# Neighbourhood attention: key windows of 23, 31, 31 and 24 columns, and the upper left tiles' keys in two blocks of partitions

## The chip, the cores and the metric

The kernel runs on one core of a Trainium2 chip. The core has five engines that run side by side, each with its own queue of instructions: TensorE (PE: matrix products and transposes into PSUM), VectorE (DVE), ScalarE (ACT), GpSimd (POOL) and SyncE (SP, which here only issues transfers). The metric is the time of one execution on the device in microseconds, lower is better; from several runs the median is taken.

## The reference

One layer of an encoder on 1024 tokens, a grid of 16 rows and 64 columns, in float32. The input is normalised and projected; half of the projected columns feed a gated convolution over positions, the other half a two-dimensional neighbourhood attention with 8 heads of 64. Both results are projected together and added to the input, and a gated feed-forward part follows. What matters here is the attention:

```python
def row_block(r):
    row_start = jnp.clip(r - kh // 2, 0, rows - kh)              # kh = 8 rows
    q_r = lax.dynamic_index_in_dim(qg, r, axis=1, keepdims=False)
    k_rows = lax.dynamic_slice_in_dim(kg, row_start, kh, axis=1)
    v_rows = lax.dynamic_slice_in_dim(vg, row_start, kh, axis=1)
    k_win = k_rows[:, :, col_idx]      # 16 columns from clip(col - 8, 0, 48)
    v_win = v_rows[:, :, col_idx]
    s = jnp.einsum("bqhd,brqchd->bhqrc", q_r, k_win) * scale
    s = s + bias                       # a learned bias for each offset
    p = jax.nn.softmax(s, axis=(-2, -1))
    return jnp.einsum("bhqrc,brqchd->bqhd", p, v_win)
```

A query in row r and column c attends to 8 rows by 16 columns, 128 keys; near the edges the window is pushed inside the grid.

## The kernel before

The layer runs in stages on one core: the input projections (keys, gate and convolution input, queries, values), the attention, the output projection, the feed-forward part's first two products and its last one. The convolution's taps run on VectorE, ScalarE and GpSimd beside TensorE's projections. The order of all instructions is the order in which the program writes them (a manual schedule); each engine takes its own in that order and waits where data or a buffer isn't there yet.

The attention takes the queries in eight tiles of 8 rows by 16 columns, 128 queries each: `rh` is the upper (0) or lower (1) half, `cb` the column block from 0 to 3. A tile's keys are a rectangle that holds the windows of all its queries: 12 rows (`AR`) from row `4 * rh` on, and the columns of `WIN[cb]`, a first column and a count. Keys outside a query's own window get a bias of -1e30 and so a weight of zero. The tiles go in the order (0,0), (1,0), (0,3), (1,3), (0,1), (1,1), (0,2), (1,2); with four pairs of heads each they make 32 units, `i` from 0 to 31. Units 0 to 3 are the upper left tile (0,0), 4 to 7 the lower left, 8 to 15 the tiles of column block 3, and 16 to 31 the wide ones of blocks 1 and 2. A unit's steps:

- `score_mm` (L646): the product of queries and keys for each of two heads, one PSUM bank each of 288 or 384 columns. In the trace that is 4 instructions, as a float32 product is two.
- `score_exp`: for each head VectorE adds the bias table and finds the maximum (L659), ScalarE takes the exponential with its sum (L661).
- `score_norm`: VectorE inverts the sums (L666), GpSimd multiplies (L668).
- `flip` (L677): TensorE transposes the weights, so that keys lie on partitions. With 288 keys that is three blocks of 96 for each head, with 384 three of 128, so 6 transposes. They go to a PSUM buffer of which there is one (`cv`).
- `flip_out` (L682): the second head's block is copied to SBUF by ScalarE, the first's by VectorE.
- `weigh` (L693): three products with the values for each head, which add up in PSUM; 12 instructions.

The loop works in a skewed order. Its step `i` issues the score of unit `i`, the normalisation of unit `i - 1`, the flip of `i - 2` and the weighing of `i - 3`. Beside these, odd steps below 19 hold four transposes of the convolution's result (L793) with its statistics (L802) and a copy (L806); steps 18 to 22 an inverse root on VectorE (L816 and on); steps 23 to 30 the scaling of the convolution's result (`conv_scale`, L824); steps 17 to 32 splits of output weights into two parts (L114, L118) and steps 15, 25 and 30 an accumulating load by GpSimd (L148). Units 0 and 1 have their scores earlier, ahead of the last two value projections (L122 to L124, `z`).

The values go to a DRAM buffer `vd` as they come, two grid rows a step (L434, issued by ScalarE). `load_vw` (L631, on SP) brings them back as one tile for each group of four rows: the rectangle's keys on partitions, 96 or 128 of them. Upper tiles use groups 0 to 2, lower ones 1 to 3. Two groups share one of 22 SBUF buffers of 4 KB a partition (`G`), which nearly everything else in the attention uses as well; a buffer that is given back goes to the next that asks.

The bias tables are built in DRAM much earlier. `t1` has one for each of three kinds of column block (left, inner, right), `tf` one for each kind and half; `fill1` and `fill2` fill them with -1e30, `run` writes the biases in runs of 16, `rows_of` copies 8 rows for a row of queries. `table` (L619, on SP) loads one for a tile.

Of the kernel before, what the change touches and what calls it, by code (L numbers as in the profile page):

```python
# [6 lines left out]
F32 = mybir.dt.float32  # L7
# [6 lines left out]
P = 128  # L14
# [4 lines left out]
NH = 8  # L19
HD = 64  # L20
# [3 lines left out]
EPS = 1e-6  # L24
NEG = -1e30
GW = 64
AR = 12
SIDE = ((16, 17, 18, 19, 20, 21, 22),) * 2 + ((16, 17, 18, 19, 20, 21, 22, 23, 24),) + (tuple(range(16, 28)),)
WIN = ((0, 24, 8), (8, 32, 0), (24, 32, 0), (40, 24, 0))


def layout(v):
# [42 lines left out]
def build(ctx, tc, a):  # L75
    nc = tc.nc
    pe, act, dve, pool = nc.tensor, nc.scalar, nc.vector, nc.gpsimd
# [3 lines left out]
    dr = ctx.enter_context(tc.tile_pool(name="dr", bufs=1, space=bass.MemoryType.DRAM))  # L81
# [4 lines left out]
    def G(name, dt=F32):  # L86
        return T("G", [P, 1024], 22, name, dt)
# [16 lines left out]
    def mm(name):  # L104
        return ps.tile([P, 512], F32, tag="mm", bufs=4, name=name)
# [142 lines left out]
    for kp in range(4):  # L248
        load_xt(0, kp, FIRST)
        if kp < 3:  # L250
# [15 lines left out]
                       base=0, channel_multiplier=1)  # L266
    qgs = T("qgs", [P, 1], 1, "qgs")
    dve.tensor_scalar(qgs, qg, HD ** -0.5, None, op0=OP.mult)
    t1 = [dr.tile([NH, 16, 15, ncol], F32, name=f"t1{ty}") for ty, ncol in enumerate((24, 32, 24))]
    tf = {(rh, ty): dr.tile([8, 16, NH, AR * t1[ty].shape[-1]], F32, name=f"tf{rh}{ty}")  # L270
          for rh in range(2) for ty in range(3)}

    def rstd_of(ss, scale, name):
# [222 lines left out]
    def bias_tables():  # L496
        neg = G("neg")
        pool.memset(neg, NEG)

        def fill1(ty):  # L500
            n = 15 * t1[ty].shape[-1]
            nc.sync.dma_start(t1[ty].rearrange("h j u b -> (h j) (u b)"), neg[:, :n])

        def fill2(rh, ty):
            n = 3 * AR * t1[ty].shape[-1] if ty != 1 else 2 * AR * 32
            for o in range(0, NH * AR * t1[ty].shape[-1], n):
                w = min(n, NH * AR * t1[ty].shape[-1] - o)
# [100 lines left out]


    def table(rh, ty):  # L610
        n = AR * t1[ty].shape[-1]
        src = tf[rh, ty].rearrange("i j h c -> (i j) (h c)")
        if rh == 0 and ty == 0:
            parts = [(G(f"tab{k}")[:, :n * min(3, NH - 3 * k)], 3 * k) for k in range(3)]
        else:
            parts = [(H(f"tab{rh}{ty}")[:, :NH * n], 0)]
        heads = []
        for w, h0 in parts:
            nc.sync.dma_start(w, src[:, h0 * n:h0 * n + w.shape[-1]])  # L619
            heads += [w[:, o:o + n] for o in range(0, w.shape[-1], n)]  # L620
        return heads
# [2 lines left out]
    vwt, vw = {}, {}  # L624

    def load_vw(cb, g):
        c0, ncol, _ = WIN[cb]
        if g % 2 == 0:
            vwt[cb, g // 2] = G(f"vw{cb}{g}").rearrange("p (g d) -> p g d", d=512)
        vw[cb, g] = vwt[cb, g // 2][:4 * ncol, g % 2, :]  # L630
        nc.sync.dma_start(vw[cb, g], vd.rearrange("(r c) d -> r c d", c=GW)[g * 4:g * 4 + 4, c0:c0 + ncol, :])  # L631


    k4 = kT.rearrange("p c (r w) -> p c r w", w=GW)
    order = [(rh, cb) for cb in (0, 3, 1, 2) for rh in range(2)]
# [2 lines left out]
    def score_mm(i):  # L638
        s_, hp = divmod(i, 4)
        rh, cb = order[s_]  # L640
        t = rh * 4 + cb
        c0, ncol, _ = WIN[cb]
        out = []
        for hh in range(2):
            s = mm(f"s{i}{hh}")[:, :AR * ncol]
            pe.matmul(s, qT[hh * HD:(hh + 1) * HD, hp, t * P:(t + 1) * P],  # L646
                      k4[hh * HD:(hh + 1) * HD, hp, rh * 4:rh * 4 + AR, c0:c0 + ncol], start=True, stop=True)
            out.append(s)
        return out

    def score_exp(i, ss):
        s_, hp = divmod(i, 4)
        rh, cb = order[s_]
        n = AR * WIN[cb][1]
        e = es[i] = G(f"e{i}").rearrange("p (h n) -> p h n", h=2)[:, :, :n]
        rs = SM(f"rs{i}", 2)
        for hh in range(2):
            mx = SM(f"mx{i}{hh}", 1)
            dve.tensor_tensor_reduce(out=e[:, hh], in0=ss[hh], in1=tab[rh, cb][2 * hp + hh], scale=-1.0,  # L659
                                     scalar=3.0e38, op0=OP.add, op1=OP.min, accum_out=mx)  # L660
            act.activation(e[:, hh], e[:, hh], AF.Exp, bias=mx, scale=-1.0, accum_out=rs[:, hh:hh + 1])  # L661
        sums[i] = rs
# [6 lines left out]

    def flip(i):  # L670
        s_, hp = divmod(i, 4)
        m = 4 * WIN[order[s_][1]][1]
        pp[i] = cv(f"p{i}")
        for hh in range(2):
            pt = pp[i][:, hh * 512:hh * 512 + 384]
            for g in range(3):
                pe.transpose(pt[:m, g * P:(g + 1) * P], es[i][:, hh, g * m:(g + 1) * m], ident)  # L677
        pTs[i] = G(f"pT{i}").rearrange("p (n h q) -> p n h q", h=2, q=P)[:m, :3]

    def flip_out(i, hh):  # L680
        m = pTs[i].shape[0]
        (dve.tensor_copy, act.copy)[hh](pTs[i][:, :, hh], pp[i][:m, hh * 512:hh * 512 + 384].rearrange(  # L682
            "p (n q) -> p n q", q=P))

    def weigh(i):
        s_, hp = divmod(i, 4)
        rh, cb = order[s_]
        if hp == 0:
            os_[s_] = tp(f"o{s_}").rearrange("p (c q) -> p c q", c=4)
        for g in range(3):  # L690
            for hh in range(2):
                c = (2 * hp + hh) * HD
                pe.matmul(os_[s_][hh * HD:(hh + 1) * HD, hp], vw[cb, rh + g][:, c:c + HD], pTs[i][:, g, hh],  # L693
                          start=g == 0, stop=g == 2)

    rowf, diff, a11 = [], [], {}

# [55 lines left out]
    load_window(3)  # L753
    tab[1, 3] = table(1, 2)

# [645 lines left out]
```

## Time and profile before

| | |
|---|---|
| median of 3 runs | 1049.9 us (1049.48 to 1050.58) |
| the profiled execution | 1050.14 us |
| its span, first to last instruction | 1048.4 us |
| TensorE busy | 1028.2 us, 98% |
| VectorE, ScalarE, GpSimd busy | 722.9, 465.3, 452.6 us |
| clock granted to TensorE | 0.999 of full |
| scores L646, flips L677, weighings L693 on TensorE | 26.73, 28.54, 28.04 us busy |

The span is what the trace covers; the execution's own time is 1.7 us longer. Times in the trace count from the span's start. The units' scores begin between 227 and 315 us, and the last weighing begins at 325. "Busy" of a group is the time in which at least one of its instructions runs: TensorE's overlap, so that the mean length of one is more than its share. "Idle before" is the time in which the engine stood still just ahead of an instruction, with what released it.

### The profile page before, as it was taken

To read this page: it belongs to the slowest core of one execution; us is meant where nothing else is said; L and a number is where in the kernel's file an instruction comes from. 1 tells how busy PE (TensorE), PEld (TensorE's weight loads), DVE (VectorE), ACT (ScalarE), POOL (GpSimd) and SP (SyncE) were. 2 spreads that over 40 slices of the span, in tenths; PEclk is the share of its full clock that TensorE was granted. 3 is DMA by queue.
4 is the path that set the end of the run, shared out by engine and by line. 5 is a ranking of instruction groups with operands and counts; after the bars stand their busy time and mean duration, and the time that the engine had idled before them with its cause. 6 is when DMAs were issued, how large, how long until landed. Compare 5 with 4: busy or idle time off the path is not lost.

```text
span 1048.4 us, 13903 instructions
## 1 busy us (share of the span) xinstructions
PE 1028.2 (98%) x4972; PEld 833.8 (80%) x4972; DVE 722.9 (69%) x1097; ACT 465.3 (44%) x915; POOL 452.6 (43%) x342
## 2 busy tenths in 40 slices
PE   7999999999999999999999999999999999999997
PEld 5888888776657888778888888888888888888885
DVE  6768998976896575876564655646556567768883
ACT  6466346636776676532232232232322443443441
POOL 0226578833575863655545454455454100002310
PEclk9999999999999999999999999999999999999999
DMA  9496771285536754465232132232232597633641
GB/s 334 178 271 220 225 238 61 77 244 168 148 109 163 159 182 141 109 167 174 104 131 101 71 131 101 89 132 93 99 111 81 207 326 256 205 101 125 215 133 40
DMA packets 74678, 162.93 MB, mean 155 GB/s; under 512 B 13489, under 2 KB 22193, under 8 KB 73905
## 3 DMA queue, kind: packets, MB, share of 16 engines
q1 hardware_dynamic: 67776, 144.14, 40.7%
q0 software_dynamic: 4864, 10.49, 5.9%
q10 hardware_dynamic: 1968, 7.42, 2.0%
q8 instruction: 39, 0.64, 0.2%
q14 instruction: 31, 0.25, 0.1%
HBM read 122.86 MB, written 53.15 MB: 168 GB/s over the span
## 4 chain that ended last, share of the span: by engine, by line
PE 88%; DVE 4%; POOL 2%; DMA 2%; ACT 2%; issue 2%; SPq 0%; POOLq 0%; ACTq 0%; DVEq 0%
PE B L122 5%; PE B L123 5%; PE B L124 5%; PE D L123 4%; PE D L124 4%; PE D L122 4%; PE A L122 3%; PE A L123 3%; PE A L124 3%; PE z L123 3%; PE z L122 3%; PE z L124 3%; PE gl L124 3%; PE gl L123 3%; PE gl L122 3%; PE n L122 3%
## 5 line engine op out<-in xcount | busy, mean ns | idle before, releaser
L347 DVE SCALAR_TENSOR_TENSOR cv<-u,par,cv 128x1009 f32<-128x1009 f32 (+14 forms) x85 | 108.5, 1276 | 2.0
L373 POOL TENSOR_TENSOR pa<-pa,pr 128x1022 f32<-128x1022 f32 (+10 forms) x31 | 75.2, 2426 | 33.7 <-ACT pr L372 32.2
L1356 POOL TENSOR_TENSOR ou<-ou,resm 128x512 f32<-128x512 f32 x8 | 12.5, 1571 | 142.5 <-DMA resm<-xd 142.5
L114 ACT CAST op<-sr 128x512 fp32r<-128x512 f32 x77 | 47.7, 619 | 52.7 <-PE B2d L124 21.3
L118 DVE TENSOR_TENSOR op<-sr,op 128x512 fp32r<-128x512 f32 x77 | 58.2, 756 | 16.4 <-ACT op L114 16.4
L1193 DVE TENSOR_TENSOR g<-B,g 128x512 f32<-128x512 f32 x22 | 15.2, 690 | 71.3 <-PE B L124 68.2
L1202 ACT ACTIVATE D<-D 128x512 f32<-128x512 f32 x22 | 12.8, 582 | 112.5 <-DVE D L1201 112.5
L1185 DVE TENSOR_TENSOR u<-B,g 128x512 f32<-128x512 f32 x22 | 15.2, 691 | 61.0 <-PE B L124 61.0
L668 POOL TENSOR_SCALAR e<-e,rs 128x288 f32<-128x288 f32 (+1 forms) x64 | 35.0, 568 | 45.6 <-DVE rs L666 41.0
L114 ACT CAST op<-wd 128x512 fp32r<-128x512 f32 x66 | 40.9, 620 | 30.4 <-DVE wd L1280 17.4
L118 DVE TENSOR_TENSOR op<-wd,op 128x512 fp32r<-128x512 f32 x66 | 50.5, 765 | 1.9 <-ACT op L114 0.3
L986 DVE TENSOR_TENSOR ts<-ts,gu 128x512 f32<-128x512 f32 x36 | 43.3, 1203 | 0.6
L1191 ACT ACTIVATE A<-A 128x512 f32<-128x512 f32 x18 | 10.5, 582 | 68.6 <-PE A L124 68.6
L661 ACT ACTIVATE e<-e,mx 128x288 f32<-128x288 f32 (+1 forms) x64 | 36.3, 569 | 2.9 <-DVE mx L659 2.8
L659 DVE CUSTOM_DVE_ANT_0 e<-s,tab 128x288 f32<-128x288 f32 (+1 forms) x64 | 29.7, 501 | 8.7 <-PE s L646 8.4
L372 ACT ACTIVATE pr<-u,par 128x1022 f32<-128x1022 f32 (+10 forms) x31 | 34.2, 1135 | 1.2 <-ACT vs L433 1.2
L677 PEld LDWEIGHTS p<-ident,e 128*96 128x96 f32 (+1 forms) x192 | 20.0, 133 | 18.1 <-POOL e L668 10.4
L677 PE MATMUL p<-ident,e 128*96 128x128 f32 (+1 forms) x192 | 28.5, 281 | 2.3 <-DVE pT L682 1.0
L986 DVE TENSOR_TENSOR ts<-gu 128x512 f32<-128x512 f32 x18 | 30.1, 1670 | 0.0
L865 DVE TENSOR_TENSOR x<-x,n 128x512 f32<-128x512 f32 x32 | 21.0, 681 | 13.1 <-PE n L124 13.1
L693 PE MATMUL o<-pT,vw 96*64 96x128 f32 (+1 forms) x384 | 28.0, 281 | 0.0
L646 PE MATMUL s<-kT,qT 64*128 64x288 f32 (+1 forms) x128 | 26.7, 495 | 0.0
(1066 smaller groups left out, 3524.1 us busy)
## 6 DMA issues: line engine op xcount, KB each, us to landing
sr<-sd SPq DMA_DIRECT2D x77, 256.0 KB
gu<-in_gu SPq DMA_DIRECT2D x36, 512.0 KB
sd<-sd SPq DMA_DIRECT2D x22, 512.0 KB
wd<-in_wd SPq DMA_DIRECT2D x44, 256.0 KB
sd<-g SPq DMA_DIRECT2D x33, 256.0 KB
x<-in_x SPq DMA_DIRECT2D x12, 512.0 KB
xd<-x SPq DMA_DIRECT2D x8, 512.0 KB
resm<-xd SPq DMA_DIRECT2D x16, 256.0 KB
```

The source lines that it names most:

```text
L114: act.copy(hi, src)
L118: eng.tensor_tensor(*[w[..., sl] for w in (lo, src, hi.bitcast(F32))], OP.subtract)
L122: pe.matmul(acc, lh, rh, start=start, stop=False, skip_group_check=True)
L123: pe.matmul(acc, lh, rl, start=False, stop=False, skip_group_check=True)
L124: pe.matmul(acc, ll, rh, start=False, stop=stop, skip_group_check=True)
L347: dve.scalar_tensor_tensor(acc[:, o], uc[:, i], dwk[:, c, t:t + 1], acc[:, o], OP.mult, OP.add)
L372: act.activation(pr[:, o], uc[:, i], AF.Copy, scale=dwk[:, c, t:t + 1])
L373: pool.tensor_tensor(pa[:, o], pa[:, o], pr[:, o], OP.add)
L661: act.activation(e[:, hh], e[:, hh], AF.Exp, bias=mx, scale=-1.0, accum_out=rs[:, hh:hh + 1])
L668: pool.tensor_scalar(es[i][:, hh], es[i][:, hh], rs[:, hh:hh + 1], 1.0, op0=OP.mult, op1=OP.mult)
L677: pe.transpose(pt[:m, g * P:(g + 1) * P], es[i][:, hh, g * m:(g + 1) * m], ident)
L986: dve.tensor_tensor(lr(tsum[i, 1])[n - 3] if o is None else o, l, r, OP.add)
```

## The change

The column counts go from 24, 32, 32, 24 to 23, 31, 31, 24. Those are the columns that the windows of 16 neighbouring query columns cover: 16 + 7 at the left edge, 16 + 15 inside, and 24 at the right edge, where the first column stays 40. The upper left tile takes 11 rows instead of 12, since the windows of rows 0 to 7 end in row 10: its keys are 11 x 23 = 253. They go in two blocks of partitions, keys 0 to 127 and 125 to 252; the first block's values have 125 rows, so no key counts twice. Its flips are 4 transposes instead of 6 and its weighings 8 instructions instead of 12.

The other tiles keep three groups, of 92 keys in the lower left tile, 96 in column block 3 and 124 in the wide ones. The upper left tile's values come in a tile of their own by four loads (keys 0 to 114, 115 to 124, 125 to 137 and 138 to 252) in place of three; the lower left tile's groups 1 to 3 are loaded after the last value step, where before only group 3 was. The left column block then takes three of the 22 buffers instead of two. The bias tables have the new widths and heights.

```diff
-AR = 12
+AR = ((11, 12, 12), (12, 12, 12))
+KIND = (0, 1, 1, 2)
-WIN = ((0, 24, 8), (8, 32, 0), (24, 32, 0), (40, 24, 0))
+WIN = ((0, 23), (8, 31), (24, 31), (40, 24))
...
-    t1 = [dr.tile([NH, 16, 15, ncol], F32, name=f"t1{ty}") for ty, ncol in enumerate((24, 32, 24))]
-    tf = {(rh, ty): dr.tile([8, 16, NH, AR * t1[ty].shape[-1]], F32, name=f"tf{rh}{ty}")
+    t1 = [dr.tile([NH, 16, 15, ncol], F32, name=f"t1{ty}") for ty, ncol in enumerate((23, 31, 24))]
+    tf = {(rh, ty): dr.tile([8, 16, NH, AR[rh][ty] * t1[ty].shape[-1]], F32, name=f"tf{rh}{ty}")
...
     def load_vw(cb, g):
-        c0, ncol, _ = WIN[cb]
-        if g % 2 == 0:
+        c0, ncol = WIN[cb]
+        if (cb, g // 2) not in vwt:
             vwt[cb, g // 2] = G(f"vw{cb}{g}").rearrange("p (g d) -> p g d", d=512)
...
+    SPLIT = 125
+    v00 = []
+
+    def load_v00(j):
+        if not v00:
+            w = G("v00").rearrange("p (g d) -> p g d", d=512)
+            v00.extend((w[:SPLIT, 0], w[:, 1]))
+        src = vd.rearrange("(r c) d -> r c d", c=GW)
+        ncol = WIN[0][1]
+        r, c = divmod(SPLIT, ncol)
+        if j == 0:
+            nc.sync.dma_start(v00[0][:r * ncol], src[:r, :ncol, :])
+            nc.sync.dma_start(v00[0][r * ncol:], src[r, :c, :])
+        else:
+            nc.sync.dma_start(v00[1][:ncol - c], src[r, c:ncol, :])
+            nc.sync.dma_start(v00[1][ncol - c:], src[r + 1:AR[0][0], :ncol, :])
+
+    def parts(rh, cb):
+        m = 4 * WIN[cb][1]
+        if rh == cb == 0:
+            return [(0, P, v00[0]), (SPLIT, SPLIT + P, v00[1])]
+        return [(g * m, g * m + m, vw[cb, rh + g]) for g in range(3)]
...
     def flip(i):
         s_, hp = divmod(i, 4)
-        m = 4 * WIN[order[s_][1]][1]
+        cuts = parts(*order[s_])
         pp[i] = cv(f"p{i}")
         for hh in range(2):
-            pt = pp[i][:, hh * 512:hh * 512 + 384]
-            for g in range(3):
-                pe.transpose(pt[:m, g * P:(g + 1) * P], es[i][:, hh, g * m:(g + 1) * m], ident)
-        pTs[i] = G(f"pT{i}").rearrange("p (n h q) -> p n h q", h=2, q=P)[:m, :3]
+            for g, (l, r, _) in enumerate(cuts):
+                o = hh * 512 + g * P
+                pe.transpose(pp[i][:r - l, o:o + P], es[i][:, hh, l:r], ident)
+        pTs[i] = G(f"pT{i}").rearrange("p (n h q) -> p n h q", h=2, q=P)[:cuts[0][1], :len(cuts)]
...
-        for g in range(3):
+        cuts = parts(rh, cb)
+        for g, (_, _, v) in enumerate(cuts):
             for hh in range(2):
                 c = (2 * hp + hh) * HD
-                pe.matmul(os_[s_][hh * HD:(hh + 1) * HD, hp], vw[cb, rh + g][:, c:c + HD], pTs[i][:, g, hh],
-                          start=g == 0, stop=g == 2)
+                pe.matmul(os_[s_][hh * HD:(hh + 1) * HD, hp], v[:, c:c + HD], pTs[i][:v.shape[0], g, hh],
+                          start=g == 0, stop=g == len(cuts) - 1)
...
-    for g in range(3):
-        load_vw(0, g)
+    for j in range(2):
+        load_v00(j)
     score_exp(0, s0)
     s1 = score_mm(1)
     value(7)
     score_norm(0)
     score_exp(1, s1)
     step()
-    load_vw(0, 3)
+    for g in range(1, 4):
+        load_vw(0, g)
```

Scores, copies and table loads take their sizes from the same constants.

More of the change, by code (lines that the diff above doesn't have):

```diff
@@ L504, in fill2 @@
         def fill2(rh, ty):
-            n = 3 * AR * t1[ty].shape[-1] if ty != 1 else 2 * AR * 32
-            for o in range(0, NH * AR * t1[ty].shape[-1], n):
-                w = min(n, NH * AR * t1[ty].shape[-1] - o)
+            one = AR[rh][ty] * t1[ty].shape[-1]
+            n = (2 if ty == 1 else 3) * one
+            for o in range(0, NH * one, n):
+                w = min(n, NH * one - o)
                 nc.sync.dma_start(tf[rh, ty].rearrange("i j h c -> (i j) (h c)")[:, o:o + w], neg[:, :w])
@@ L610, in table @@
     def table(rh, ty):
-        n = AR * t1[ty].shape[-1]
+        n = AR[rh][ty] * t1[ty].shape[-1]
         src = tf[rh, ty].rearrange("i j h c -> (i j) (h c)")
@@ L641, in score_mm @@
         t = rh * 4 + cb
-        c0, ncol, _ = WIN[cb]
+        c0, ncol = WIN[cb]
         out = []
         for hh in range(2):
-            s = mm(f"s{i}{hh}")[:, :AR * ncol]
+            s = mm(f"s{i}{hh}")[:, :AR[rh][KIND[cb]] * ncol]
             pe.matmul(s, qT[hh * HD:(hh + 1) * HD, hp, t * P:(t + 1) * P],
-                      k4[hh * HD:(hh + 1) * HD, hp, rh * 4:rh * 4 + AR, c0:c0 + ncol], start=True, stop=True)
+                      k4[hh * HD:(hh + 1) * HD, hp, rh * 4:rh * 4 + AR[rh][KIND[cb]], c0:c0 + ncol], start=True, stop=True)
             out.append(s)
@@ L653, in score_exp @@
         rh, cb = order[s_]
-        n = AR * WIN[cb][1]
+        n = AR[rh][KIND[cb]] * WIN[cb][1]
         e = es[i] = G(f"e{i}").rearrange("p (h n) -> p h n", h=2)[:, :, :n]
@@ L671, in flip @@
         s_, hp = divmod(i, 4)
-        m = 4 * WIN[order[s_][1]][1]
+        cuts = parts(*order[s_])
         pp[i] = cv(f"p{i}")
         for hh in range(2):
-            pt = pp[i][:, hh * 512:hh * 512 + 384]
-            for g in range(3):
-                pe.transpose(pt[:m, g * P:(g + 1) * P], es[i][:, hh, g * m:(g + 1) * m], ident)
-        pTs[i] = G(f"pT{i}").rearrange("p (n h q) -> p n h q", h=2, q=P)[:m, :3]
+            for g, (l, r, _) in enumerate(cuts):
+                o = hh * 512 + g * P
+                pe.transpose(pp[i][:r - l, o:o + P], es[i][:, hh, l:r], ident)
+        pTs[i] = G(f"pT{i}").rearrange("p (n h q) -> p n h q", h=2, q=P)[:cuts[0][1], :len(cuts)]
     def flip_out(i, hh):
-        m = pTs[i].shape[0]
-        (dve.tensor_copy, act.copy)[hh](pTs[i][:, :, hh], pp[i][:m, hh * 512:hh * 512 + 384].rearrange(
+        m, n = pTs[i].shape[:2]
+        (dve.tensor_copy, act.copy)[hh](pTs[i][:, :, hh], pp[i][:m, hh * 512:hh * 512 + n * P].rearrange(
             "p (n q) -> p n q", q=P))
```

## Prediction

> **What bounds the kernel now.** The page's first part comes first, then the chain of waits in order of time through the attention (239 to 317 us), the same stretch cut into stages, and the waits of TensorE there. The page:
>
> ```profile
> span 1048.4 us, 13903 instructions
> PE 1028.2 (98%) x4972; PEld 833.8 (80%) x4972; DVE 722.9 (69%) x1097; ACT 465.3 (44%) x915; POOL 452.6 (43%) x342
> ```
>
> TensorE is busy 98%, but that is an average over stages. The chain of waits (start, us, what) shows the stage that is changed:
>
> ```profile
> 239.79 0.69 PE s L646 x4
> 240.48 0.81 PE p L677 x6
> 241.36 0.48 ACT pT L682
> 241.87 0.57 DVE pT L682
> 242.57 0.83 PE p L677 x6
> 243.40 0.44 PE y L793 x4
> 243.84 0.81 PE o L693 x12
> 244.64 0.69 PE s L646 x4
> 245.33 0.79 PE p L677 x6
> 246.12 0.81 PE o L693 x12
> ...
> 274.66 0.84 PE s L646 x4
> ...
> 299.00 0.82 PE p L677 x6
> ```
>
> One unit (a tile and two heads) is a score of 4 instructions (L646), a flip of 6 transposes (L677) and a weighing of 12 (L693): 0.69 + 0.79 + 0.81 = 2.29 us, and 0.44 more where the convolution's transposes (L793) stand between. The reader sees one gap, from 241.29 to 242.57, where the second flip waits for the copies of the first; from 242.57 on TensorE follows TensorE. By stages (columns PE, PEld, DVE, ACT, POOL, clock, DMA share, GB/s):
>
> ```profile
> 250.00:260.00 10.00, 10.00 (x100) 7.08 (x96) 7.45 (x29) 7.75 (x24) 3.95 (x8) 1.00 0.94 274
> 300.00:310.00 10.00, 9.18 (x82) 5.36 (x78) 9.90 (x27) 7.67 (x23) 7.91 (x13) 1.00 0.50 107
> ```
>
> In the narrow tiles (units 0 to 15) TensorE is full and the others have a quarter to spare. In the wide ones (16 to 31) VectorE is at 9.90 of 10 and TensorE has gaps. Its waits, first from 239 to 280 us and then from 280 to 317:
>
> ```profile
> PE p L677 <- DVE pT L682: 0.6, 1, 0.6
> ```
>
> ```profile
> PE p L677 <- POOL e L668: 0.9, 4, 0.3
> PE p L677 <- DVE pT L682: 0.4, 1, 0.4
> PE p L677 <- DVE rcq L816: 0.3, 1, 0.3
> ```
>
> So removed TensorE work counts in full up to unit 15, and the wide half holds 0.9 + 0.4 + 0.3 = 1.6 us of waits that can shrink or grow.
>
> **The change part by part.** Units 0 to 3 (upper left tile) go from 288 keys to 253 in two blocks; units 4 to 7 from 288 to 276; the 16 wide units from 384 to 372; units 8 to 15 stay.
>
> *Scores.* 384 against 288 columns is 0.84 against 0.69, so 0.15 / 96 = 1.56 ns a column. 35 columns in 4 units are 0.22 us, 12 in 4 units 0.07, 12 in 16 units 0.30: 0.59 us. Scores 0 and 1 stand among the projections, where the chain is TensorE as well, so nothing is taken off.
>
> *Flips.* A transpose with 128 columns takes 0.82 / 6 = 0.137 us on the chain, so four take 0.55 where six of 96 took 0.79: 0.24 in each of 4 units, 0.97 us. For 124 columns instead of 128 the chain's slope (0.82 - 0.79 over 32 columns) gives 0.004 a flip, 0.06 over 16.
>
> *Weighing.* 12 instructions in 0.81 become 8: 0.27 in each of 4 units, 1.08 us. That 125 and 128 rows cost what 96 do is seen in the groups, where the two shapes take the same:
>
> ```profile
> L693 PE MATMUL o<-pT,vw 96*64 96x128 f32 x192 | 14.0, 281 | 0.0
> L693 PE MATMUL o<-pT,vw 128*64 128x128 f32 x192 | 14.0, 281 | 0.0
> L661 ACT ACTIVATE e<-e,mx 128x384 f32<-128x384 f32 x32 | 19.4, 609 | 0.9 <-DVE mx L659 0.8
> L661 ACT ACTIVATE e<-e,mx 128x288 f32<-128x288 f32 x32 | 16.8, 529 | 2.0 <-DVE mx L659 2.0
> L659 DVE CUSTOM_DVE_ANT_0 e<-s,tab 128x384 f32<-128x384 f32 x32 | 16.4, 549 | 0.2
> L659 DVE CUSTOM_DVE_ANT_0 e<-s,tab 128x288 f32<-128x288 f32 x32 | 13.3, 452 | 8.5 <-PE s L646 8.4
> L668 POOL TENSOR_SCALAR e<-e,rs 128x288 f32<-128x288 f32 x32 | 15.8, 505 | 43.0 <-DVE rs L666 38.3 <-PE s L646 2.4 <-PE p L677 2.2
> ```
>
> *Do the other engines keep up in units 0 to 3?* TensorE's unit there becomes 0.635 + 0.55 + 0.54 = 1.72 us, 2.16 with the convolution's transposes, 1.94 on average. A unit now costs VectorE 7.45 / 4 = 1.86 and ScalarE 1.94 (four units in the stage 250 to 260). From the rows above a column costs ScalarE 0.83 ns and VectorE 1.01; 35 columns less in two exponentials and two maxima, and 128 less in each copy, leave 1.77 and 1.66. Both fit, ScalarE by 0.17. Two loops are tighter. Flip to flip through both copies: 241.29 to 242.57 is 1.28, less 0.11 and 0.13 for the shorter copies is 1.04; with the flip 1.59, under 1.72. The softmax loop (maximum, two exponentials, reciprocal, next maximum):
>
> ```profile
> 240.51 0.46 DVE L659 CUSTOM_DVE_ANT_0 e<-s,tab 128x288 f32<-128x288 f32 x1 [4.46 <-PE s L646]
> 241.74 0.53 ACT L661 ACTIVATE e<-e,mx 128x288 f32<-128x288 f32 x1
> 242.91 0.17 DVE L666 RECIPROCAL rs<-rs 128x2 f32<-128x2 f32 x1 [0.49 <-ACT e L661]
> 243.03 0.46 DVE L659 CUSTOM_DVE_ANT_0 e<-s,tab 128x288 f32<-128x288 f32 x1
> ```
>
> From the first exponential to the next maximum is 1.29, with the first maximum (it hands over after about 0.4) 1.7, and 1.6 after the change; but with a copy of the flip in front on ScalarE it nears 2.0, just over TensorE's average. Over four units this can cost 0.1 each, 0.3 in all. Against it the first gap shrinks from 1.28 - 0.69 = 0.59 to 1.04 - 0.635 = 0.40. The net is between -0.3 and +0.2; I take 0, between these ends. From unit 4 on TensorE needs about 2.5 a unit again and the cover returns.
>
> *Loads of values.* Three loads become four for the upper tile, and the lower one's three now follow the last value step, in a third of the 22 shared buffers.
>
> ```profile
> 233.19 0.60 SPq L631 DMA_DIRECT2D vw<-vd  x1
> ```
>
> ```profile
> 242.62 0.60 SPq L631 DMA_DIRECT2D vw<-vd  x1
> ```
>
> ```profile
> SPq L631 <- DMA vd<-vs: 23.5, 3, 8.9
> ```
>
> The first row is the last load that unit 0's weighing (243.84) needs; it waits for a value store, as its successor will (rows 6 to 10 end in the same token block). The lower tile's last load, at 242.62, waits for the last store before and after. Two added loads at 0.60 fit between, and weighing 0 keeps its 10 us. The loads for the first wide tile, from 250 us on, do wait for a buffer:
>
> ```profile
> SPq L631 <- POOL e L668: 9.0, 1, 9.0
> ```
>
> ```profile
> 265.65 2.42 SPq L619 DMA_DIRECT2D tab<-tf  x1
> ```
>
> The added buffer goes back after unit 3's weighing, before most of that wait, so the count is as before. The last table stands behind those loads on SP (265.65) and is first used in unit 20, four units after the score at 274.66: some 15 us of cover. Cost: nothing, ends 0 and 0.3. If the 10 us went, unit 0's weighing would be late by what is missing.
>
> *Tables.* Rows of 23 and 31 entries shrink tables and their loads by 3 to 12%; each is loaded ahead of its use, the last as just shown. Nothing.
>
> *The wide half.* TensorE's 0.02 a unit is counted above; VectorE gains 2 x 12 x 1.01 = 0.024 a unit, so it holds the pace where VectorE sets it. Its 1.6 us of waits depend on how engines meet; I take no change, with ends of 1.6 won and 1.6 lost.
>
> **Sum:** 0.59 + 0.97 + 0.06 + 1.08 = 2.7 us. The profiled execution took 1050.14 us (its span is 1048.4); less 2.7 is 1047.4. The median of the runs, 1049.9, lies 0.24 below that execution, so I predict 1047.2.
>
> **The rivals.**
> *Ragged rows cost full rows.* TensorE reads the keys in runs of 23 or 31; no row here has a run that isn't a multiple of 8. If a run costs what 24 or 32 did, only the twelfth key row of the upper left tile is saved: 24 x 1.56 ns x 4 = 0.15 us of scores instead of 0.59. The gain is 2.3, the time 1047.6. Speaking for it: nothing in the trace; against: nothing either. [...]
>
> *GpSimd dislikes 253.* The normalisation (L668, 0.505 for 288) has no row with an odd count. If it took twice as long, 2 us for both heads, flip 2 would come about 0.4 late in each of four units, 1.6 in all: gain 1.1, time 1048.8, no change. For: the odd length is new; against: GpSimd is idle 6 of 10 us there, so it takes a factor near two before it counts.
>
> *Slower: the convolution's scaling meets GpSimd.* In units 23 to 30:
>
> ```profile
> L824 DVE TENSOR_SCALAR xh<-xh,par x8: 532/664/2330, 295.6 to 314.6; 128x512 f32<-128x512 f32 x8
> ```
>
> Eight equal instructions take from 532 to 2330 ns. Moved by a few tenths against GpSimd's work they can fall differently. From the median row to the longest is 1.67. Two more of the longest, 3.3, use up the gain (1050.5); it decides from three on, 5.0 less 2.7, which gives 1052.2. Against: VectorE's end there is only in part on the chain. [...]
>
> **How the numbers follow.** Likeliest, 0.60: all as summed, 1046.2 to 1048.2 by the ends above that touch it. Ragged rows 0.12 (1047.6). GpSimd, or the wide half's waits eating what is won, 0.21 (1048 to 1050). Slower 0.07. A difference under 0.2% (2.1 us) can't be told from no change here, so "faster" begins at 1047.8: most of the first two cases, 0.64; the same 0.29; slower 0.07. The range is 1045.6 (all 1.6 us of waits won) to 1049.4.
>
> **What would show it.** Score rows of 253 and 372 columns at 0.635 and 0.82 on the chain, flips of 4 at 0.55, weighings of 8 at 0.54, unit 7's score at about 249.5 instead of 251.86, and unit 31's near 311.6 instead of 314.22, which stand now at:
>
> ```profile
> 251.86 0.76 PE L646 MATMUL s<-kT,qT 64*128 64x288 f32 x4
> ```
>
> ```profile
> 314.22 0.92 PE L646 MATMUL s<-kT,qT 64*128 64x384 f32 x4
> ```
>
> Wrong would be: a wait of TensorE on GpSimd or on the copies in each of the first units, chain rows of 0.69 for 253 columns, unit 0's weighing waiting for a load, or the scaling instructions near 2 us.

## The result and the profile after

The changed kernel takes 1047.51 us (median of 12 runs, 1047.02 to 1048.74); the kernel before takes 1050.33 (12 runs, 1049.26 to 1050.85). The ratio is 0.9976, with a 95% interval of 0.9967 to 0.9985. The profiled execution took 1047.52 us. Its page:

```profile
span 1045.8 us, 13866 instructions
PE 1026.0 (98%) x4948; PEld 831.7 (80%) x4948; DVE 721.7 (69%) x1097; ACT 464.4 (44%) x915; POOL 450.7 (43%) x342
```

TensorE has 24 instructions and 2.2 us less to do, and the span is 2.6 shorter. The changed program is longer, so its line numbers differ: L671 is the score, L702 the flip, L719 the weighing, L684 the maximum, L693 the normalisation, L820 the convolution's transposes; they move by a few more lines in some of the kernels below. The chain of waits (start, us, what) where the kernel before had 0.69, 0.79 and 0.81:

```profile
239.11 0.63 PE s L671 x4
...
241.97 0.44 PE y L820 x4
242.40 0.59 PE o L719 x8
242.99 0.67 PE s L671 x4
243.66 0.58 PE p L702 x4
244.24 0.59 PE o L719 x8
244.83 0.67 PE s L671 x4
...
247.11 0.67 PE s L671 x4
247.78 0.79 PE p L702 x6
248.57 0.59 PE o L719 x8
249.16 0.67 PE s L671 x4
```

Scores of 253 columns (L671) take 0.63 and of 276 columns 0.67, flips of 4 (L702) 0.58, weighings of 8 (L719) 0.59. The last row is unit 7's score; in order of instructions it starts at 249.09, and before at 251.86. TensorE's waits, from 239 to 280 us and from 280 to 317:

```profile
PE p L702 <- DVE pT L707: 0.4, 1, 0.4
```

```profile
PE p L702 <- POOL e L693: 0.9, 4, 0.3
PE p L702 <- DVE pT L707: 0.4, 1, 0.4
PE p L702 <- DVE rcq L843: 0.3, 1, 0.3
```

The first gap is 0.2 shorter; the wide half's 1.6 us are the same three waits of the same length. Two of the groups by shape (GpSimd's normalisation) and, in order of time, the last score:

```profile
L693 POOL TENSOR_SCALAR e<-e,rs 128x253 f32<-128x253 f32 x8 | 3.7, 480 | 24.8 <-DVE rs L691 19.0 <-PE p L702 5.7
L693 POOL TENSOR_SCALAR e<-e,rs 128x288 f32<-128x288 f32 x16 | 7.9, 503 | 11.3 <-DVE rs L691 6.7 <-PE s L671 2.4 <-PE p L702 2.2
```

```profile
311.24 0.90 PE L671 MATMUL s<-kT,qT 64*128 64x372 f32 x4
```

Set against before in order of time, the starts of TensorE's scores tell where the 2.6 us between the two profiled spans come from; how much earlier than before a unit starts is called its lead. Unit 0 starts 0.61 early (226.38 against 226.99), unit 8 2.71, unit 16 2.71, unit 31 2.98 (311.24 against 314.22). So the attention gave 2.37: 2.1 in units 0 to 7, nothing in 8 to 15, 0.26 in the wide half. The 0.61 ahead of unit 0 is not the change's: TensorE's work up to there is the same, its first projection starts 0.7 us earlier (6.6 against 7.3), and the other kernels below begin unit 0 between 0.67 early and 0.47 late. Between 442 and 452 us 0.73 is given back, and the stretch behind the last matmul is 0.38 shorter: 0.61 + 2.37 - 0.73 + 0.38 = 2.63.

### The profile page after: what moved, and what is told of

It is laid out like the page before. It is cut to its first block, busy times and chain, and to the rows that moved or that the text cites. A ratio compares the mean times of both kernels' runs of the same rounds, so it can differ in the third digit from the quotient of the medians.

```text
span 1045.8 us, 13866 instructions
## 1 busy us (share of the span) xinstructions
PE 1026.0 (98%) x4948; PEld 831.7 (80%) x4948; DVE 721.7 (69%) x1097; ACT 464.4 (44%) x915; POOL 450.7 (43%) x342
## 4 chain that ended last, share of the span: by engine, by line
PE 88%; DVE 3%; issue 3%; POOL 2%; ACT 2%; DMA 1%; SPq 0%; POOLq 0%; ACTq 0%; DVEq 0%
PE B L124 5%; PE B L125 5%; PE B L123 5%; PE D L124 4%; PE D L125 4%; PE D L123 4%; PE A L124 3%; PE A L125 3%; PE A L123 3%; PE z L124 3%; PE z L123 3%; PE z L125 3%; PE gl L125 3%; PE gl L123 3%; PE gl L124 3%
## 5 line engine op out<-in xcount | busy, mean ns | idle before, releaser
L119 DVE TENSOR_TENSOR op<-sr,op 128x512 fp32r<-128x512 f32 x77 | 56.1, 728 | 15.2 <-ACT op L115 15.1
L693 POOL TENSOR_SCALAR e<-e,rs 128x372 f32<-128x372 f32 (+3 forms) x64 | 34.3, 557 | 43.8 <-DVE rs L691 33.4
L686 ACT ACTIVATE e<-e,mx 128x372 f32<-128x372 f32 (+3 forms) x64 | 35.6, 559 | 2.9 <-DVE mx L684 2.7
L684 DVE CUSTOM_DVE_ANT_0 e<-s,tab 128x372 f32<-128x372 f32 (+3 forms) x64 | 28.9, 489 | 8.8 <-PE s L671 8.0
L702 PEld LDWEIGHTS p<-ident,e 128*124 128x124 f32 (+3 forms) x184 | 19.2, 134 | 17.5 <-POOL e L693 10.2
L702 PE MATMUL p<-ident,e 128*124 128x128 f32 (+3 forms) x184 | 27.6, 281 | 2.1 <-POOL e L693 0.9
L671 PE MATMUL s<-kT,qT 64*128 64x372 f32 (+3 forms) x128 | 26.1, 485 | 0.0
L123 PE MATMUL B2d<-op 128*128 128x512 f32 x66 | 25.8, 391 | 0.0
```

The costliest lines, as they stand in the source:

```text
L119: eng.tensor_tensor(*[w[..., sl] for w in (lo, src, hi.bitcast(F32))], OP.subtract)
L123: pe.matmul(acc, lh, rh, start=start, stop=False, skip_group_check=True)
L693: pool.tensor_scalar(es[i][:, hh], es[i][:, hh], rs[:, hh:hh + 1], 1.0, op0=OP.mult, op1=OP.mult)
L702: pe.transpose(pp[i][:r - l, o:o + P], es[i][:, hh, l:r], ident)
```

## The experiments

The first theory, A, is the prediction's sum: TensorE's own work counts in full, everything else is hidden. The rivals were ragged rows at the cost of full ones, a schedule that falls anew, and a cost that doesn't go by the number of instructions. Each ratio is to the kernel before, run beside it, and a distance to before is that of these two medians; leads are from one profiled execution.

**The columns alone** (kernel before, 12 rows and three blocks everywhere).

```
-WIN = ((0, 24, 8), (8, 32, 0), (24, 32, 0), (40, 24, 0))
+WIN = ((0, 23, 8), (8, 31, 0), (24, 31, 0), (40, 24, 0))
```

> The kernel before with columns 23, 31, 31, 24 alone: 12 key rows and three blocks in every tile, loads as before. Theory A (TensorE's work sets the attention's pace, and every column counts): the narrow left units save 12 columns at 1.56 ns each, 8 x 0.019 = 0.15 us, the wide ones 16 x 0.019 = 0.30, flips 0.06: the last score comes 0.5 us earlier against the projections before it, the time 0.4 to 0.6 below before. Rival B (the gain is in the narrower columns, through VectorE in the wide half): more than 1.5 us of the 2.6 appear here. Rival C (ragged rows cost full rows): no change in the score rows on the chain, 0.69 and 0.84.

Measured: 1049.95 us against 1050.5, ratio 0.9994 (0.9985 to 1.0002). The time alone doesn't tell that from no change. The scores do: unit 0 is 0.35 early, unit 16 0.52, unit 31 0.85, so the columns give 0.17 on the left and 0.33 in the wide half. On the chain a score of 276 columns (23 x 12) and one of 372 (31 x 12) take:

```profile
244.22 0.67 PE s L646 x4
274.14 0.82 PE s L646 x4
```

Twelve columns fewer at 1.56 ns are 0.02 us, and 0.69 and 0.84 became 0.67 and 0.82: a run of 23 or 31 words cost what its words cost.

**Wide columns back at 32** (changed kernel).

```
-WIN = ((0, 23), (8, 31), (24, 31), (40, 24))
+WIN = ((0, 23), (8, 32), (24, 32), (40, 24))
```

> The changed kernel with 32 columns in the two inner column blocks; the left column keeps 23 columns, 11 rows and two blocks in its upper tile. Theory A: loses only the wide half's 0.26 us that the trace after shows between unit 16's score and unit 31's, so 2.2 to 2.5 us below before. Rival B: at most 1.1 us below before. The wide half's waits of TensorE (0.9, 0.4 and 0.3 us) come out the same, and the eight scaling instructions have the same lengths in the same order, if it is only moved; a redraw would change them.

Measured: 1047.94 us, ratio 0.9977 (0.9968 to 0.9987). Up to unit 21 as theory A has it; then one step, from unit 21 to 22, takes 3.46 instead of 2.76 us, and the lead falls from 2.26 to 1.56. VectorE's and TensorE's waits from 280 to 292 us, and the maximum of unit 20:

```profile
DVE e L684 <- DMA tab<-tf: 0.6, 1, 0.6
```

```profile
PE p L702 <- DVE rcq L843: 1.0, 1, 1.0
```

```profile
285.36 0.56 DVE L684 CUSTOM_DVE_ANT_0 e<-s,tab 128x384 f32<-128x384 f32 x1 [0.60 <-DMA tab<-tf]
```

The bias table of the lower wide tiles, the last one on SP, comes too late. This kernel's nine executions fall into two groups, five from 1047.5 to 1047.9 and four from 1048.5 to 1048.7, and the profiled one is of the second. That fits a table that is late in some executions and not in others; the first group has no profile.

**Eleven rows in all upper tiles** (changed kernel; the right and wide upper tiles load rows 7 to 10 once more, in an extra buffer).

```
-AR = ((11, 12, 12), (12, 12, 12))
+AR = ((11, 11, 11), (12, 12, 12))
```

> The changed kernel with 11 key rows in all four upper tiles: 264 keys in the right one and 341 in the inner ones, still three blocks, the second weighed with three rows of keys and the third holding rows 7 to 10, which takes one more load and one more of the 22 buffers for each column block. Theory A: scores save 24 x 1.56 ns x 4 + 31 x 1.56 ns x 8 = 0.15 + 0.39 us, so 0.5 below the changed kernel. Rival D (buffers): from step 14 on the exponentials' buffer is the one of two units before, which is given back by the flip of the same step; VectorE's maximum then starts about 0.8 us later in steps 14 to 17, TensorE waits there, and the kernel is not faster than the changed one, up to 2 us slower.

Measured: 1053.55 us, ratio 1.0029 (1.0018 to 1.0039), 3.05 us slower than before. Units 8 to 12 gain 0.04 each as expected, units 14 to 20 lose some 0.4 to the buffers, and the step from unit 21 to 22 takes 7.86 us. SP's queue and the maximum of unit 20:

```profile
249.97 19.57 SPq L634 DMA_DIRECT2D vw<-vd  x5
269.64 5.15 SPq L621 DMA_DIRECT2D tab<-tf  x1
```

```profile
288.52 0.55 DVE L688 CUSTOM_DVE_ANT_0 e<-s,tab 128x372 f32<-128x372 f32 x1 [3.85 <-DMA tab<-tf]
```

Neither theory as put: the table again, 3.85 us late behind five value loads. The stages behind that wait (the clock stands third from last, before DMA share and GB/s) show a second price:

```profile
286.00:290.00 4.00, 0.11 (x2) 0.00 (x0) 1.48 (x6) 0.89 (x3) 0.00 (x0) 0.85 0.25 101
290.00:292.00 2.00, 1.84 (x10) 1.54 (x12) 1.93 (x10) 0.93 (x4) 1.23 (x2) 0.50 0.26 100
292.00:294.00 2.00, 2.00 (x16) 1.25 (x12) 1.27 (x7) 1.71 (x6) 0.81 (x3) 0.50 0.48 132
```

TensorE stood still for 4.05 us and was then granted half its clock; the clock's records have it at half from 288.8 to 295.6.

**One block in the upper left tile** (its first 125 keys are left out of flips and weighings).

```
-            return [(0, P, v00[0]), (SPLIT, SPLIT + P, v00[1])]
+            return [(SPLIT, SPLIT + P, v00[1])]
```

> The changed kernel, whose upper left tile flips and weighs only its second block; keys 0 to 124 are left out of the weighing there, so the output of these queries is not the reference's. Flips are 2 transposes and weighings 4 instructions in units 0 to 3. Theory P (as predicted: a group costs in proportion): 0.27 and 0.27 us on the chain. Theory F (each group has a fixed start of 0.11 and 0.15 us, from 6 transposes in 0.82 and 4 in 0.585, 12 instructions in 0.81 and 8 in 0.59): 0.35 and 0.37 us. If TensorE still set the pace, units 1 to 4 would take 1.4 us, 1.8 with the convolution's transposes. The loop through the maximum, the exponentials and the copies was put at about 1.9 to 2.0 us: then TensorE waits in these units for the copies or the normalisation, and the step from score 3 to score 7 is near 7.6 us rather than 6.4.

Measured: 1047.13 us, ratio 0.9967 (0.9955 to 0.9979). From score 3 to 7 it takes 7.51 us where TensorE's work alone would take 6.4 (estimated from the group times): with TensorE's share cut again, the other engines' loops bind. From unit 8 it leads by 3.17, and in the step from 21 to 22 it loses 0.84 to the same table.

So theory T: the table is the next bound, because it is issued behind four value loads. The next four kernels move it ahead of the last two of them:

```
+        if i == 6:
+            for g in (0, 1):
+                load_vw(1, g)
+            book_vw(1, 2)
         if i == 9:
             tab[1, 1] = tab[1, 2] = table(1, 1)
-        if i in (6, 18):
-            load_window(1 + i // 18)
+            for g in (2, 3):
+                load_vw(1, g)
+        if i == 18:
+            load_window(2)
```

(`book_vw` takes the buffer without a load.)

**On the changed kernel:**

> The changed kernel with the last bias table issued earlier: of the four value loads of the third column block, two go out in unit 6 and two only behind the table, in unit 9 (the buffers are booked as before). Theory T (in the two runs in which unit 20 or 21 waited for this table, the table's packets stood behind all four value loads on the few DMA engines that carry those loads): SP should issue the table at about 256 instead of 264.9, its last large packets should land some 8 to 10 us earlier than 282.4, and since the changed kernel does not wait for it, the time stays within 0.3 us of the changed kernel's, with unit 8 at 251.8 to 252.0 and unit 31 at 311.1 to 311.4. Rival U (the table was already costing the changed kernel something that the waits do not show, or the later value loads come too late for unit 16's weighing): the time moves by 0.5 us or more either way, and the step from unit 21 to 22 or a wait of the weighing on a value load shows it.

Measured: 1047.48 us, ratio 0.9969 (0.9958 to 0.9981), 2.83 below before where the changed kernel is 2.82 below. Units 8 and 31 stand a microsecond behind the places expected (252.90 and 312.23), since this execution began unit 0 that much later. The SP queue:

```profile
247.93 5.35 SPq L636 DMA_DIRECT2D vw<-vd  x2
253.37 9.92 SPq L621 DMA_DIRECT2D tab<-tf  x1
263.39 19.76 SPq L636 DMA_DIRECT2D vw<-vd  x6
```

By the trace's DMA records the table's last large packet ends at 277.3 instead of 283.4, six us earlier and not eight to ten. In the changed kernel unit 20's maximum starts at 284.15, so the packet was only 0.8 ahead of it; in the wide-32 kernel it ended at 284.6 and the maximum that waited for it began 0.7 later. By that, an estimate, the cover left in the changed kernel is about 0.1 us. This is also a second profile of the changed attention: unit 0 is 0.47 late, unit 31 1.99 early, a gain of 2.46.

**On the wide-32 kernel:**

> The changed kernel with the wide columns back at 32, and the last table issued ahead of the last two value loads of its column block. Theory T: the step from unit 21 to 22, 3.46 us with the table late, comes back to 2.75, the wait of the maximum for the table (0.6) and of the flips for the maximum (1.0) are gone, and the time falls by 0.7 to about 2.9 to 3.3 us below the kernel before. Rival V (the step is long for another reason, such as the start of the square-root loop or the second wide tile's buffers): the step stays at 3.4 to 3.5 and the time within 0.2 of the earlier run's distance of 2.6 us.

Measured: 1047.61 us, ratio 0.9974 (0.9963 to 0.9985). The step is 2.76 again, unit 31 leads by 2.79, and of TensorE's waits from 280 to 292 us one is left:

```profile
PE p L705 <- DVE rcq L846: 0.3, 1, 0.3
```

So theory T holds for the step. The time does not follow it: the distance to before is 2.7 us, below the 2.9 to 3.3 expected and within 0.2 of the earlier 2.6, as rival V had it. Five of the nine earlier executions had already been near it (1047.5 to 1047.9), which fits a table that was not late in them.

**On the one-block kernel:**

> The kernel whose upper left tile flips and weighs only its second block (the first 125 keys are left out of the flips and the weighings), with the last table issued ahead of the last two value loads. Theory T: unit 8 is unchanged at 3.1 to 3.2 us ahead of the kernel before, the step from unit 21 to 22 falls from 3.60 to 2.75, and the lead stays at 3.2 to 3.5 us to unit 31 instead of falling to 2.4 to 2.6; the time is 4.0 to 4.3 us below the kernel before where it was 3.4. Rival V: step and lead as in the earlier run.

Measured: 1046.16 us against 1050.31, ratio 0.9958 (0.9941 to 0.9974). The step from 21 to 22 is 2.73, the lead grows from 3.62 (unit 8) to 3.93 (unit 31). As theory T for the step, the growth and the time; the leads are above those expected, of which 0.25 is an earlier unit 0. The chain of this kernel also has the short groups:

```profile
242.33 0.67 PE s L674 x4
242.99 0.37 PE p L705 x2
243.36 0.37 PE o L722 x4
```

Two transposes take 0.37, four weighings 0.37.

**On the kernel with eleven rows:**

> The kernel with 11 rows in all upper tiles, with the last table issued behind three instead of five value loads. Theory T: the step from unit 21 to 22 falls from 7.86 us to 3 or less, the wait of 3.8 us for the table goes, and 5.1 us come back: 1.5 to 2.3 us below the kernel before, still above the changed kernel by the 0.3 to 0.9 us that units 16 to 20 lose to the two extra buffers. Rival W (the five value loads keep the queue and the few DMA engines busy so long that whatever stands behind them is late): the value loads that are now behind the table come late instead, unit 16 or 20 waits for them by 1 us or more, and no more than half of the 5.1 us comes back.

Measured: 1056.69 us, ratio 1.0058 (1.0043 to 1.0073), worse than without the move. The wait for the table is down to 0.4 and the step from 21 to 22 is 2.58, but unit 26 to 27 takes 11 us. GpSimd and TensorE from 285 and from 295 us on, and a stage after it:

```profile
POOL P31r L149 <- DMA P31r<-in_w: 6.8, 1, 6.8
```

```profile
PE p L710 <- POOL e L701: 7.4, 2, 7.2
```

```profile
308.00:310.00 2.00, 2.00 (x16) 1.34 (x16) 0.99 (x2) 1.50 (x5) 1.04 (x3) 0.50 1.01 195
```

A weight block that SP issues behind the value loads (at 292.2; at 288.2 in the changed kernel with the table moved) is late, GpSimd waits for it with the normalisations queued behind, and TensorE, after 7.2 us of idle time, again comes back at half clock. Theory T has the step right and the time wrong; rival W is right in kind: what stands behind five value loads is late, but it was the transfer after the ones named.

**Weighings in pairs.** The groups pointed to a fixed start that joined groups would save; on the left alone, and everywhere.

```
-            weigh(i - 3)
+            if i >= 19:        # i >= 33 in the second kernel
+                weigh(i - 3)
+            elif i % 2 == 0:
+                weigh(i - 4)
+                weigh(i - 3)
```

> The changed kernel with the weighings of two neighbouring units issued one behind the other in the second unit's turn, for units 0 to 15 alone; nothing is left out. Theory F (a group of matmuls has a fixed start: weighing groups of 4, 8 and 12 took 0.369, 0.589 and 0.806 us, which is 0.15 + 0.0547 each): every pair that is joined saves 0.15 us of TensorE, so two steps of units 8 to 15 together go from 5.00 to 4.85 us, and seven or eight pairs give 1.0 to 1.2 us: unit 16 at 3.7 to 3.9 us ahead of the kernel before instead of 2.7, the time 1.0 below the changed kernel's. Rival P (cost goes by the number of matmuls, and the first one's slowness is only that of the loads before it): 0 to 0.2 us. Rival L (the turns become uneven, 1.9 and 2.9 us, and the loop over maximum, exponential and scaling, some 2.0 us a unit, does not follow): the short steps come out at 2.1 or more and half of the gain or more is lost.

> The same pairing of weighings for all units up to 29 instead of up to 15. Theory F: seven more pairs, up to 1.0 us more than the kernel that pairs the left units only, 1.9 to 2.2 us below the changed kernel. Rival L: in the wide units the turns become 1.6 and 3.2 us, while VectorE needs 2.0 and more for each (its stretch from 300 to 310 us is busy for 9.96 of 10 us); the short turns then wait for the maximum, and nothing or less than nothing is gained beyond the left units: unit 31 no further ahead, against its place in the kernel paired on the left, than 0.3 us, or behind it.

Measured: 1047.86 us, ratio 0.9980 (0.9971 to 0.9989), and 1047.76, ratio 0.9977 (0.9969 to 0.9986): no gain over the changed kernel in either. The chain of the first one:

```profile
252.84 1.46 PE o L719 x24
254.30 0.69 PE s L671 x4
254.99 0.81 PE p L702 x6
...
255.82 0.48 ACT pT L707
...
256.32 0.55 DVE pT L707
```

A weighing of 24 takes 1.46, as theory F has it (0.15 + 24 x 0.0547). But two steps of units 8 to 15 take 5.01 to 5.07 us, not 4.85. The short one takes 1.91, as theory F has it, and not 2.1 or more as rival L; the long one takes 3.16 instead of 2.94, since without a weighing between two flips the second waits for the copies of the first, which share one PSUM buffer. TensorE's waits of that kind from 239 to 317 us are 1.3 in the first kernel and 2.3 in the second, against 0.7. Most of what the joining saves, the cover that it took away costs. The table has a part in it too: unit 20's maximum waited for it by 0.5 us in the first kernel and 0.3 in the second, and the step from unit 21 to 22 of the first one is 3.21 instead of 2.77. Without that wait it would be, by an estimate from the leads, some 0.2 ahead of the changed kernel, counted from unit 0.

**What gives 0.7 back at 442 to 452 us.** The trace of the changed kernel there, VectorE and GpSimd:

```profile
438.91 5.50 DVE L1060 TENSOR_TENSOR s<-xT,sn 128x256 f32<-128x256 f32 x2
```

```profile
439.10 1.21 POOL L1028 DMA_DIRECT2D gum<-in_g  x1 [0.67 <-DVE S L119]
439.90 1.74 POOL L119 TENSOR_TENSOR t1m<-gum,t1m 128x512 fp32r<-128x512 f32 x1
441.16 1.71 POOL L119 TENSOR_TENSOR t0m<-gum,t0m 128x512 fp32r<-128x512 f32 x1
442.41 1.70 POOL L119 TENSOR_TENSOR t1m<-gum,t1m 128x512 fp32r<-128x512 f32 x1
```

One of the two VectorE instructions took 5.16 us, usually 0.41, and ended 0.3 after GpSimd's run. In the kernel before the same happened one instruction later (4.54 for 0.68), where less stood behind it. So it did in eight of the ten kernels above (of the two with eleven rows it is not shown), among them the changed one with its table moved, which gives back 0.12. What is given back there is 0.1 to 0.5 in these kernels, so it differs from one execution to the next and is not set by the change.

```
-                pool.dma_start(*later.pop(n_prep[1]), accum_op=OP.add)
+                d, more = later.pop(n_prep[1])
+                n_acc.append(1)
+                if len(n_acc) != 2:
+                    pool.dma_start(d, more, accum_op=OP.add)
```

> The changed kernel without the second accumulating transfer that GpSimd issues in the feed-forward stage (one block's sum is left out; everything else as before). Theory G (a two-input VectorE instruction that starts next to an unbroken run of GpSimd instructions is held until the run ends): the run there, 1.21 us of transfer and three subtractions, shrinks by the 0.8 us that lay ahead of the first subtraction; the VectorE instruction caught there takes 4.1 to 4.4 us instead of 4.5 to 5.2 and still ends within 0.4 us of GpSimd's last subtraction. Rival H (VectorE waits for something else, such as the transfer itself or its own input): its length stays at 4.5 to 5.2, or falls to 0.4 to 0.7 with the transfer gone.

Measured in one execution: 1047.5 us. Neither as put: VectorE's instructions there take 1.5 to 1.8 us, each ending 0.3 to 0.6 after the end of one GpSimd subtraction, and nothing is given back (TensorE's lead grows from 2.1 to 2.4). So with the transfer gone the long hold is gone, and VectorE gets in at the ends of single GpSimd instructions. The run of three subtractions was broken up as well in this execution; whether such a run holds VectorE without a transfer is not shown. That pointed to a version with nothing left out:

```
-                    later[n_prep[1] + 2] = (d, more[0])
+                    later[n_prep[1] + 3] = (d, more[0])
```

> The changed kernel with each of GpSimd's accumulating transfers in the feed-forward stage issued one subtraction later; nothing is left out. Theory G2 (the long hold of a VectorE instruction, 4.5 to 5.2 us, comes with an accumulating transfer right ahead of three subtractions that are ready; apart from it VectorE gets in at the end of each GpSimd instruction, 1.5 to 1.8 us): if the transfer no longer opens such a run, no VectorE instruction between 436 and 450 us takes over 2.5 us, nothing is given back there (in the changed kernel 0.65 us), and the time is 0.3 to 1.1 us below the changed kernel's. Rival K (the hold goes with the run of subtractions, wherever the transfer stands): an instruction of 3.5 us or more is found again, if another one, and the time is within 0.3 us of the changed kernel's, or above it where the transfer now stands before work that TensorE waits for.

Measured: 1049.03 us, ratio 0.9989 (0.9979 to 0.9998), 1.3 us above the changed kernel by the distance to before. The hold is gone as theory G2 has it (no VectorE instruction there over 2.3 us), but the shifted transfers make an operand late: ScalarE's cast of such a block waits 0.41 us for its transfer, VectorE's two instructions behind take 2.36 us beside GpSimd instead of 1.82, and TensorE's operand comes 1.0 later. Its instructions in order of time, and two stages:

```profile
436.27 0.39 PE L125 MATMUL B<-S,t0m 128*128 128x512 f32 x1
439.16 0.77 PE L123 MATMUL B<-S,t1m 128*128 128x512 f32 x1 [2.50 <-DVE u L1212]
439.72 0.63 PE L124 MATMUL B<-S,t1m 128*128 128x512 f32 x1
440.15 0.63 PE L125 MATMUL B<-S,t1m 128*128 128x512 f32 x1
```

```profile
434.00:438.00 4.00, 2.66 (x12) 1.88 (x10) 2.91 (x3) 2.30 (x5) 4.00 (x4) 1.00 0.37 123
438.00:442.00 4.00, 2.84 (x7) 2.29 (x8) 4.00 (x4) 0.41 (x1) 4.00 (x4) 0.62 0.19 57
```

The idle time there is 2.50 us instead of 1.47 (changed kernel), and after it the matmuls start every 0.43 us instead of 0.23, for three microseconds. The profiled execution is the fastest of the eleven (1047.93), so what the median lost beyond it is not shown. Of the kernels that leave nothing out, none beats the changed one by more than the measurement can tell.

## Why the prediction was right, and where its steps were not

The time, 1047.5 for 1047.2 predicted, is right, and the mechanism is shown: TensorE's removed work counts, up to unit 15 in full, and the wide half keeps its pace. Against the marks: unit 7's score at 249.09 (249.5 predicted), unit 31's at 311.24 (311.6). Both are some 0.4 early by a start-up (all that stands ahead of unit 0) that was 0.6 early; from unit 0 on the gain is 2.37 for 2.7. That the time is as close as 0.3 is in part luck, as the terms below and the last paragraph say.

*Scores:* 0.06 in each of units 0 to 3 and 0.02 in each of 4 to 7, as predicted; the wide half 0.26 to 0.33 for 0.30 + 0.06. Right.

*Flips:* 0.97 predicted, 0.82 measured (from one group's start to the next's, 0.79 to 0.585). *Weighings:* 1.08 predicted, 0.87 measured (0.806 to 0.589). These two terms were 0.36 too large by one error: the cost of a group was divided by its count. Start to start, weighings of 4, 8, 12 and 24 take 0.369, 0.589, 0.806 and 1.461, which is 0.15 + 0.0547 n; flips of 2, 4 and 6 take 0.368, 0.585 and 0.79, which is 0.15 + 0.107 n within 0.01 (the six have 96 keys a block, the others 128). The start stayed when instructions went.

*Other engines in units 0 to 3:* taken as 0 between -0.3 and +0.2. The first gap shrank by 0.2 (from 0.62 to 0.39 in order of time), as worked out, and TensorE shows no other wait there: +0.2, at the end of the range. That the loops were near is shown by the one-block kernel, where they bind.

*Loads of values:* nothing, right but for 0.07: a maximum of VectorE at 248.36 waited 0.5 us for a value load, and the lead falls by 0.07 from unit 7 to 8; in the kernel with the table moved neither is there. *Tables:* "some 15 us of cover" was wrong. The working took the time of issue for the time of arrival; the last table's packets end at 283.4, 18 us after it is issued, and unit 20's maximum reads it at 284.15. Cover was 1.0 us before (packet end 285.3 and 0.7 more, maximum at 286.94) and 0.1 after: each microsecond won ahead of unit 20 moves the maximum toward the table. It cost nothing here only because the gain ended at 2.7 and the table's own load moved up by two.

*The wide half:* "no change" is right; the eight scaling instructions took 723, 540, 2316, 531, 736, 541, 587 and 1615 ns, before 724, 539, 2330, 532, 751, 537, 605 and 1634. They start 2.8 to 3.0 us earlier with the same lengths in the same order, so the slower rival fell.

*Ragged rows:* fell, 0.63 for 253 columns and 0.67 for 276 on the chain, and 0.50 us from the columns alone. For TensorE's reads of runs of 23 and 31 words no run here shows a cost beyond that of their words. *GpSimd dislikes 253:* fell, 480 ns for 253 and 503 for 288.

So the attention gave 2.4 of the 2.7: 0.36 less from flips and weighings, 0.2 back from the first gap, and 0.2 less in the wide half and at unit 8. The medians lie 2.82 apart. What fills the other 0.4 is not settled: the start-up and the stretches behind the attention differ by up to a microsecond from one profiled execution to the next, also where that code is the same, and the ratio's interval, 1.6 to 3.5 us, holds both numbers. The prediction also took its 2.7 from 1049.9, the median of three runs; the twelve beside the changed kernel have 1050.33.

## What to carry to other kernels

Price a group of short matmuls by a fixed start and a slope (for the weighings here 0.15 us and 0.0547 an instruction), from two groups of different size, before counting what fewer of them save; and look at what the group covers before it is joined or shortened. For a transfer take cover from its last packet, not from its issue (18 us apart for the last table of the changed kernel): whoever speeds up a stage moves its reader toward it. Where the bound engine gains, list the transfers that are next due, and queue the one with the least cover ahead of those that have more.

## What the hardware showed that was not expected

*TensorE came back slow after 2.5 us of idle time.* After 1.47 us (changed kernel) and 1.48 us (the second transfer left out) it went on at full clock; after 2.50 us it went on at 0.43 us a matmul instead of 0.23, with the clock at half from 439.0 to 442.4; after 4.05 us (eleven rows) it was at half until 295.6, for 5.5 us of work. What happens between 1.48 and 2.50 us is not shown. The stall of 4 us thus cost some two more: from unit 21 to 23 the kernel with eleven rows loses 6.1 us, of which 3.85 are the wait.

*VectorE behind a run of GpSimd.* An addition or subtraction of two SBUF inputs took 4.3 to 5.2 us (the kernel before, the changed one and eight of the others) instead of 0.4 to 0.7 when it met an accumulating transfer with three subtractions queued behind it, and 1.5 to 1.8 beside single ones (the second transfer left out). In the changed kernel the one of 5.16 us began at 439.24, lasted through all three subtractions (439.90 to 444.11) and ended 0.3 after the last. What holds it is not shown.

*The value loads used a quarter of the DMA engines.* In the changed kernel from 283 to 287 us, with little but value loads (four rows of the key grid each) on the way, the DMA share is 0.25:

```profile
283.00:287.00 4.00, 3.70 (x36) 2.48 (x37) 3.90 (x17) 2.68 (x9) 2.65 (x5) 1.00 0.25 99
```

This is why a table behind them is late though most engines are free, and the DMA records show it: four packets are under way at a time there, and of the last table's 128 large packets 96 are through by 273.7, while the other 32, a quarter, start only at 279.0 and go four at a time to 283.4. From 268 to 273 us, where the first 96 pass, a mean of 4.19 value packets (2 KB each) and 11.95 of the table's are under way. Why the value loads keep to a quarter is not shown.
